# Add and GELU on one core: y's wide rest issued from ScalarE's queue, beside x's first half in SyncE's

## The chip, the cores and the metric

The kernel runs on one core of a Trainium2 chip. The metric is device time in microseconds (us). The kernel before takes 120.19 us (median of 3 runs, 120.18 to 120.26).

## The reference

```python
batch, dim = 1024, 4096          # x, y: float32
z = x + y
return 0.5 * z * (1 + np.tanh(np.sqrt(2 / np.pi) * (z + 0.044715 * z ** 3)))
```

Two arrays of 16.8 MB are read and one is written, 50.33 MB in all.

## The kernel before

**Layout.** Each array is spread over 128 partitions with 32,768 float32 columns each (`TOT`), in two halves of 16,384 columns (`HALF`). A half of an array is one contiguous 8.39 MB block of memory, in which each partition owns a row of 64 KB. In SBUF there is a tile `zt` for all of x, in which z and the result are made in place, and a tile `yt` that holds one half of y at a time. The second half of y goes into the same place as the first, so it can be loaded only when all adds of the first half are done.

**Transfers.** Seven DMAs move everything. x comes in two halves. y comes as a narrow first piece of 704 columns (352 KB), a wide rest of its first half (15,680 columns, 7840 KB), and the second half. The output goes out in two halves. All seven are issued by SyncE, in this order, which is the list `sp` (line 178):

```python
sp = [(load_y, 0), (load_y, 1), (load_x, 0), (load_x, 1), (load_y, 2)]
sp += [(store, i) for i in range(len(stores))]
```

The first four wait for nothing. `load_y(2)` waits for the adds of the first half, each store for the GELUs of its half. After the program is compiled, `begin_early(nc, 2)` moves SyncE's first two DMAs ahead of the barrier with which the body of the program begins.

**Compute.** The columns are cut into 20 chunks. For each, x and y are added (`add`, line 159) and GELU is applied (`gelu`, line 171). Chunks 0 to 8 are the first half. VectorE does most adds, and GpSimd chunks 7, 8 and 12. For eight chunks ScalarE first copies x into PSUM (`copy`, line 152), and VectorE's add reads it from there; PSUM has room for two chunks of 2048 columns, so a later copy waits until the add of an earlier chunk has read its place. The order on each engine is written out by hand: ScalarE's is `on_scalar` (line 107), five copies of the first half, two GELUs, three copies of the second half, and then the other GELUs. The loop at line 200 emits the instructions from these queues in turn; it doesn't reorder a queue.

Before the queues, a one-element activation on ScalarE (line 199) loads the GELU table.

Of the kernel before, what the change touches and what calls it, by code (L numbers as in the profile page):

```python
# [66 lines left out]
def kernel(  # L67
# [12 lines left out]
    nc = tc.nc  # L80
# [10 lines left out]
    def rows(array, lo, hi):  # L91
        flat, at = array.rearrange("n d -> (n d)"), 0
        for f, e in blocks:
            if f <= lo and hi <= e:
                own = flat[P * at : P * (at + e - f)].rearrange("(p c) -> p c", p=P)
                return own[:, lo - f : hi - f]
            at += e - f
        raise AssertionError((lo, hi))
# [8 lines left out]
    on_scalar = [("copy", c) for c in (2, 3, 4, 5, 6)] + [("gelu", 0), ("gelu", 1)] + [("copy", c) for c in (9, 10, 11)] + [("gelu", c) for c in range(2, 20)]  # L107
# [21 lines left out]
    yt = pool_y.tile([P, HALF], fp32, tag="y", name="y")  # L129
# [11 lines left out]
    def load_y(i):  # L141
        a, b = yr[i]
        o = a % HALF
        nc.sync.dma_start(out=yt[:, o : o + b - a], in_=rows(y, a, b))  # L144

    def store(i):
        a, b = sr[i]
# [25 lines left out]
    def earlier_user(c):  # L173
        lo, hi = copies[c], copies[c] + chunks[c]
        before = [k for k in copies if k < c and copies[k] < hi and copies[k] + chunks[k] > lo]
        return [(add, k) for k in before]

    sp = [(load_y, 0), (load_y, 1), (load_x, 0), (load_x, 1), (load_y, 2)]
    sp += [(store, i) for i in range(len(stores))]
    pool = [(add, c) for c in on_gpsimd]  # L180
    dve = [(add, c) for c in on_vector]
    acts = [(gelu if what == "gelu" else copy, c) for what, c in on_scalar]

    needs = {
        load_x: lambda i: [],
# [1 line left out]
        copy: lambda c: [(load_x, i) for i in over(xr, *cr[c])] + earlier_user(c),  # L187
        add: lambda c: [(load_x, i) for i in over(xr, *cr[c])]
        + [(load_y, i) for i in over(yr, *cr[c])]
        + [(copy, k) for k in copies if k == c]  # L190
        + [(add, k) for h, k in held.items() if h == c],
# [55 lines left out]
```

## Time and profile before

| | |
|---|---|
| median of 3 runs | 120.19 us |
| the profiled execution | 120.31 us |
| its span, first to last instruction | 118.8 us |
| DMA queues that carry data | 1, 98.5% of 16 engines' span |
| mean rate over the span | 424 GB/s |
| VectorE, ScalarE, GpSimd busy | 29.1, 44.1, 13.8 us |
| y's narrow piece, issue to landing | 3.0 us |
| y's wide rest, issue to landing | 21.7 us |
| x's first half landed | 41.47 us from the span's start |
| y's second half issued, landed | 55.02, 80.14 us |
| first store issued | 77.33 us |

The busy times of the compute engines are a third of the span or less; times in the table from the third block on are counted from the span's start or from the issue of the DMA, as said. A DMA's time from issue to landing includes the time in which it stands behind others in its queue.

### The profile page before, as it was taken

The page shows a single profiled execution, that of the slowest core. Times are in us where ns is not written, and L with a number is a line of the kernel's source. Part 1 is how long each engine was busy: PE and PEld are TensorE (multiplying, and loading weights), DVE is VectorE, ACT ScalarE, POOL GpSimd, SP SyncE. Part 2 cuts the span into 40 slices and gives each one's busy share as a digit, 9 for nine tenths or more (in the row PEclk, how much of TensorE's full clock was granted, in tenths as well). Part 3 has the DMA queues.
Part 4 walks back from the last instruction along what each step waited for, and adds up shares of the span by engine and source line. Part 5 has one row for each costly group of instructions (what it writes and reads, how often), then busy time and mean ns, then how long its engine had stood idle before and what let it go on. Part 6 is the DMA issues. An engine that isn't in the chain of part 4 may idle for free.

```text
span 118.8 us, 115 instructions
## 1 busy us (share of the span) xinstructions
DVE 29.1 (24%) x18; ACT 44.1 (37%) x30; POOL 13.8 (12%) x7
## 2 busy tenths in 40 slices
DVE  0000000000000099994000000009999930000000
ACT  4000000000000096893049999903799990000000
POOL 0000000000000019980000000009500000000000
DMA  9779977998889988998899888998899888988891
GB/s 459 338 338 422 591 338 338 507 552 353 353 353 662 397 353 353 574 485 353 353 441 618 353 353 353 640 419 353 353 552 507 353 353 353 706 353 353 353 640 66
DMA packets 1008, 50.33 MB, mean 424 GB/s; under 512 B 112, under 2 KB 112, under 8 KB 240
## 3 DMA queue, kind: packets, MB, share of 16 engines
q1 hardware_dynamic: 1008, 50.33, 98.5%
HBM read 33.55 MB, written 16.78 MB: 424 GB/s over the span
## 4 chain that ended last, share of the span: by engine, by line
DMA 55%; DVE 14%; ACT 10%; DVEq 1%; ACTq 0%; issue 0%; SPq 0%
DMA z<-in_x_dram 34%; DMA y<-in_y_dram 21%; DVE z L159 14%; ACT z L171 10%; DVEq L214 1%; ACTq L214 0%; DVEq L159 0%; SPq L144 0%
## 5 line engine op out<-in xcount | busy, mean ns | idle before, releaser
L171 ACT ACTIVATE z<-z 128x2048 f32<-128x2048 f32 (+3 forms) x20 | 29.7, 1555 | 5.4 <-DVE z L159 5.4
L152 ACT COPY ps<-z 128x2048 f32<-128x2048 f32 (+2 forms) x8 | 13.0, 1654 | 47.0 <-DMA z<-in_x_dram 45.3
L159 DVE TENSOR_TENSOR z<-z,y 128x2048 f32<-128x2048 f32 (+2 forms) x9 | 13.6, 1571 | 40.2 <-DMA z<-in_x_dram 40.2
L159 DVE TENSOR_TENSOR z<-ps,y 128x2048 f32<-128x2048 f32 (+2 forms) x8 | 15.6, 2014 | 25.3 <-DMA y<-in_y_dram 25.3
L159 POOL TENSOR_TENSOR z<-z,y 128x2048 f32<-128x2048 f32 x3 | 13.5, 4533 | 70.8 <-DVE z L159 43.6
L199 ACT ACT_TABLE_LOAD x1 | 1.3, 1283 | 1.3 <-PEq L231 1.3
L198 DVE MEMSET one<- 128x1 f32 x1 | 0.1, 59 | 1.3 <-PEq L231 1.3
L199 ACT ACTIVATE one<-one 128x1 f32<-128x1 f32 x1 | 0.2, 202 | 0.0
L231 POOL MEMSET const-float32-0.0<- 128x1 f32 x1 | 0.1, 99 | 0.2 <-issue 0.2
L231 POOL MEMSET const-bfloat16-1.0<- 128x1 bf16 x1 | 0.1, 102 | 0.0
L231 POOL MEMSET const-uint8-127<- 128x1 uint8 x1 | 0.1, 102 | 0.0
L231 POOL MEMSET const-float32-1.0<- 128x1 f32 x1 | 0.1, 99 | 0.0
## 6 DMA issues: line engine op xcount, KB each, us to landing
y<-in_y_dram SPq DMA_DIRECT2D x1, 7840.0 KB, 21.7
y<-in_y_dram SPq DMA_DIRECT2D x1, 352.0 KB, 3.0
z<-in_x_dram SPq DMA_DIRECT2D x2, 49.7
out_dram<-z SPq DMA_DIRECT2D x2, 21.6
y<-in_y_dram SPq DMA_DIRECT2D x1, 25.1
```

The source lines that it names most:

```text
L152: nc.scalar.copy(out=in_psum(c), in_=zt[:, a:b])
L159: ins = eng.tensor_add(out=zt[:, a:b], in0=first, in1=yt[:, o : o + b - a])
L171: nc.scalar.activation(out=zt[:, a:b], in_=zt[:, a:b], func=act.Gelu_apprx_tanh)
L198: nc.vector.memset(one[:, :1], 0.0)
L199: nc.scalar.activation(out=one[:, :1], in_=one[:, :1], func=act.Gelu_apprx_tanh)
L214: tc.compile()
L231: nc = _bacc.Bacc("TRN2", target_bir_lowering=False, num_devices=1)
```

## The change

`load_y(1)`, the wide rest of y's first half, is taken out of SyncE's list and put at the head of ScalarE's, and it is issued from ScalarE's DMA queue. There it follows the one-element activation of line 199 and precedes the first PSUM copy. SyncE's list now begins with y's narrow piece and x's first half, and these are the two that `begin_early` moves ahead of the barrier. All sizes, chunks, waits of the adds and the order of the compute stay as they are.

```diff
     def load_y(i):
         a, b = yr[i]
         o = a % HALF
-        nc.sync.dma_start(out=yt[:, o : o + b - a], in_=rows(y, a, b))
+        queue = nc.scalar if i == 1 else nc.sync
+        queue.dma_start(out=yt[:, o : o + b - a], in_=rows(y, a, b))
 
...
-    sp = [(load_y, 0), (load_y, 1), (load_x, 0), (load_x, 1), (load_y, 2)]
+    sp = [(load_y, 0), (load_x, 0), (load_x, 1), (load_y, 2)]
     sp += [(store, i) for i in range(len(stores))]
     pool = [(add, c) for c in on_gpsimd]
     dve = [(add, c) for c in on_vector]
-    acts = [(gelu if what == "gelu" else copy, c) for what, c in on_scalar]
+    acts = [(load_y, 1)] + [(gelu if what == "gelu" else copy, c) for what, c in on_scalar]
```

## The prediction

> **What bounds the kernel now.** I read the page from part 3 on, then the chain of waits, the timeline and a table of windows cut at the landings.
>
> ```profile
> DMA packets 1008, 50.33 MB, mean 424 GB/s; under 512 B 112, under 2 KB 112, under 8 KB 240
> q1 hardware_dynamic: 1008, 50.33, 98.5%
> ```
>
> One queue carries everything, and its packets fill 98.5% of 16 engines' span. The counts give the size of a piece. Seven DMAs on 16 engines have 112 small completion packets; 240 - 112 = 128 are the narrow first DMA of y; 1008 - 240 = 768 are left for six wide DMAs, 128 each, 8 for each engine.
>
> ```profile
> 41.50 0.05 DVEq L159
> 41.60 13.36 DVE z L159 x7
> 55.02 25.12 DMA y<-in_y_dram
> 84.85 11.86 ACT z L171 x7
> ```
>
> From the chain in order of time I take three landings and one issue. x's first half has landed at 41.47 (the wait before the adds ends there), the seven VectorE adds run to 54.96, y's second half is issued at 55.02 and lands at 80.14. The chain view calls these 13.36 us of DVE a part of the critical chain, but they lie beside x's second half, as the timeline of waits shows:
>
> ```profile
> 46.20 1.87 ACT L152 COPY ps<-z 128x2048 f32<-128x2048 f32 x1 [1.03 <-DVE z L159]
> 60.91 3.76 ACT L152 COPY ps<-z 128x512 f32<-128x512 f32 x3 [6.52 <-DMA z<-in_x_dram]
> 77.33 20.78 SPq L148 DMA_DIRECT2D out_dram<-z  x2
> ```
>
> ScalarE waits 6.52 us until x's second half has landed (about 60.83). So y's second half, issued at 55.02, stands in the queue for up to 5.8 us, and the first store, issued at 77.33, stands behind it for up to 2.8 us. The compute sets when y's second half can be issued, but not when it arrives. The windows say the same in bytes. I cut them at the landings: 3.0 and 0.42 + 21.7 from the DMA issue rows, 41.47 and 80.14 from the chain, 60.83 as ScalarE's wait ends at 60.91 less a hand-over of 0.08, and for the first store twice the issue row's median of 21.6 less the second store's 21.0, so 22.2 after 77.33.
>
> ```profile
> 3.00:22.14 19.14, 0.00 (x0) 0.00 (x0) 0.00 (x0) 1.00 0.99 422
> 22.14:41.47 19.33, 0.00 (x0) 0.00 (x0) 0.00 (x0) 1.00 1.00 434
> 41.47:60.83 19.36, 13.35 (x7) 11.21 (x7) 9.02 (x2) 1.00 1.00 433
> 60.83:80.14 19.31, 0.00 (x0) 16.39 (x10) 0.00 (x0) 1.00 1.00 434
> 80.14:99.48 19.34, 15.69 (x10) 15.01 (x11) 4.53 (x1) 1.00 1.00 434
> ```
>
> From one landing to the next it is 19.3 us per 8192 KB, whatever runs beside it, the last column in GB/s. Only the first window is off pace: its 7840 KB should take 7840/8192 x 19.33 = 18.50 us and take 19.14, an excess of **0.64 us**. That excess and the first microseconds are all the slack the transfers have. A piece is 19.33/8 = **2.42 us**.
>
> **The change, part by part.** SyncE loses one issue. Its rows are 0.33 to 0.42 us each. The first two DMAs of SyncE are hoisted ahead of the entry barrier; they were both of y's, and become y's narrow one and x's first half. So x's first half is issued at about 0.4 instead of 1.25, and x's second half at 1.25 instead of about 1.66. Neither is worth anything: the 16 engines have y's narrow DMA in hand until about 3.0 and 19 us of x behind it, so no engine is idle for want of an issue.
>
> ScalarE gains one issue, 0.33 to 0.42 us, behind the warm-up activation, whose row ends at 2.55 + 0.20 = 2.75. Queued behind it is the first PSUM copy, which waits for x's first half anyway: "ACT L152 COPY ... [38.75 <-DMA z<-in_x_dram]". Cost 0; uncovered it would be 0.4 us. The DMA waits for no semaphore.
>
> Next, when y's wide rest lands. From issue to landing y's narrow DMA took 3.0 us, of which its 352 KB are 0.83 us at pace, so the lag is at most 2.17. Issued by 3.2, the wide rest has its first piece ready between 3.2 and 5.3, while x's first half starts behind the narrow DMA at 2.2 to 3.0. x thus leads by one or two pieces of 2.42 us. If engines then take turns piece by piece, a lead of one means x's first half lands near 39 and y's rest near 41.5; a lead of two lets one piece of x's second half in ahead of y's last one: y lands at 41.47 + 2.42 = 43.9. If they share byte by byte, y's 0.34 MB fewer make up most of the lead and it lands between these. The adds need both, so they start 0 to 2.42 us later. ScalarE's first two copies are then done early, which saves nothing, since the VectorE row (13.36 us without a gap) is already limited by its own adds. GpSimd's two adds shift with them and end 1.9 us before VectorE (53.06 against 54.96).
>
> The delay ends at y's second half: issued at 55.0 to 57.4, with at most 2.17 lag it is ready by 59.6, and x's second half still lands at 60.83 because the same bytes have gone before it. Slack left: at least 60.83 - 59.6 = 1.2 us. ScalarE's slack falls from 6.52 to at least 4.1. Everything after 60.83 is unchanged.
>
> A rule of the Trainium skill bears on the taking of turns. "DMA: Bandwidth & Descriptors", section "Queues, rings and completion order", says that each DMA engine goes round-robin between queues and switches only at packet boundaries. Nothing in this trace shows it, as it has one data queue; by it, with a piece as a packet, the sum is the one above.
>
> What the sharing does to the pace is the one price that no row shows. The nearest rows bound it: 434 GB/s in the windows of x, 422 in the window of y. Bounded below: the excess of 0.64 goes away, -0.64. Bounded above: both streams run as y's did, x's 19.33 us gain 0.67 more; or twice that for two switches per pair, 1.3. I take 0, by the five windows that hold pace whichever tensor and direction they carry.
>
> Sum: 0 (SyncE) + 0 (ScalarE) + 0 (delay inside the slack) + 0 (pace) on the profiled execution: 120.31, of which 118.8 is the span and 1.5 lies around it. The median of the runs is 0.12 below that execution, so the forecast is 120.2. A second queue could also need setting up outside the span; no row shows that, and I put it at 0 as well.
>
> **The rivals.** *The excess goes (faster).* x's pieces now begin the stream and y's come between them. If the excess belongs to y's wide rest being read alone, up to 0.64 goes: 119.55; half of it gives 119.9. For it: only that DMA is off pace, and x's, y's second half and both stores are not. Against it: it is also the first wide DMA of the run, and whatever starts the stream may pay the same.
>
> *The sharing costs pace (slower).* Every engine alternates between two tensors for 38 us. At y's excess for both streams: +0.67, 120.9; at double that 121.5. It decides from 0.24 us on, that is 0.24/16 = 15 ns per piece over 16 pieces, little beside 2420 ns. For it: the transfers bound the kernel everywhere, so each lost nanosecond is seen at the end. Against it: 434 GB/s held while engines passed from one DMA to the next. The Trainium skill has a rule in this direction: the same page, section "Latency and other measured facts", reports that DMA rows at a pitch of a large power of two can run at half rate. No run here shows that for two tensors; the 64 KB pitch inside one tensor runs at 434.
>
> *y's rest lands too late (slower).* If x's queue has three or more pieces committed when y's arrive, y's rest is 4.84 us late or more, and y's second half misses its place: ready at 55.02 + 4.84 + up to 2.17 = 62.0, so up to 1.2 us of idle engines; with four pieces up to 3.6. That gives 121.4 to 123.8. It decides when the adds start over 3.6 to 5.8 us late. For: nothing in the trace says how deep an engine commits. Against: the lead is a matter of 1 to 3 us by the issue rows.
>
> *One queue is emptied before the other (slower, and the change then doesn't run the two side by side).* x's second half stands behind the first in SyncE's queue from 2 us on. If the engines stay with that queue, y's rest comes after both and lands at 60.83; adds to 74.3; y's second half issued at 74.4 with nothing else to move, landing at 74.4 + 19.33 + 2.1 = 95.8 instead of 80.14: about 15.7 more, 135.9. By the Trainium skill's account on the same page a packet may hold up to 64 descriptors; x's two halves are 18 pieces with their completions, so it does not exclude this. If turns are taken whole DMA by whole DMA instead, y merely trades places with x's first half, lands at 41.5, and nothing changes; that belongs to the forecast.
>
> **How the numbers follow.** No change 0.40; excess goes 0.20; pace lost 0.26; late rest 0.09; one queue first 0.05. A difference under 0.2% (0.24 us) is about what a measurement of this kernel cannot tell from no change. The first case is within it, the second faster, the other three slower: 0.20, 0.40, 0.40. The likeliest single case gives 120.2, its own range 119.95 to 120.45. Eight in ten need the second and third cases with their bounds: 119.6 to 121.6, which leaves out the late and the one-queue case and a little of the third.
>
> **What would show it.** Right: two data queues in part 3; ScalarE's first copy waits for x near 39, the first VectorE add for y's rest between 41.4 and 44; y's second half issued by 57.5; landings near 60.8 and 80.1; all windows after that at 434 GB/s. The excess going shows as x's second half landing near 60.2. Lost pace shows as its landing after 61.1 with no idle DMA slice. A late rest shows as a DMA slice well under 9 tenths near 61 us. One queue first shows as adds that begin after 60. Wrong would be a difference that arises after 61 us or outside the span.

## The result and the profile after

The changed kernel takes 120.97 us (median of 5 runs, 120.91 to 121.42) against 120.25 for the kernel before beside it: a ratio of 1.0069, 95% interval 1.0057 to 1.0080, so **0.7 us slower**. The time lies in the forecast's range, and it went the way of the slower cases; the likeliest single case, no change, did not happen. The profiled execution is the slowest of the five, 121.42 with a span of 119.9, so its rows overstate the typical loss by about 0.4 us.

Part 3 of the page shows the second queue, with y's wide rest in it:

```profile
DMA packets 1008, 50.33 MB, mean 420 GB/s; under 512 B 112, under 2 KB 112, under 8 KB 240
q1 hardware_dynamic: 864, 42.30, 82.1%
q10 hardware_dynamic: 144, 8.03, 15.5%
```

The timeline of the changed kernel, the rows at which something is issued or a transfer awaited (start, duration, instruction, idle time before it and what ended that):

```profile
1.43 0.37 ACTq L145 DMA_DIRECT2D y<-in_y_dram  x1
39.21 3.67 ACT L153 COPY ps<-z 128x2048 f32<-128x2048 f32 x2 [36.46 <-DMA z<-in_x_dram]
44.05 2.36 DVE L160 TENSOR_TENSOR z<-z,y 128x1024 f32<-128x1024 f32 x2 [42.67 <-DMA y<-in_y_dram]
57.48 0.33 SPq L145 DMA_DIRECT2D y<-in_y_dram  x1
60.92 3.76 ACT L153 COPY ps<-z 128x512 f32<-128x512 f32 x3 [4.07 <-DMA z<-in_x_dram]
77.34 21.87 SPq L149 DMA_DIRECT2D out_dram<-z  x2
```

x's first half is there at 39.2 and y's wide rest at 43.9. The adds begin 2.45 us later than before, y's second half is issued at 57.48 instead of 55.02, and ScalarE's slack before x's second half falls from 6.52 to 4.07. So far it is what a lead of two pieces was to give. x's second half also lands where it did (60.84; 60.83 before). The windows, cut at the landings of this kernel, show where the time went:

```profile
2.89:39.19 36.30, 0.00 (x0) 0.00 (x0) 0.00 (x0) 1.00 0.99 423
39.19:43.93 4.74, 0.00 (x0) 3.67 (x2) 0.00 (x0) 1.00 1.02 442
43.93:60.84 16.91, 13.35 (x7) 7.54 (x5) 9.02 (x2) 1.00 0.99 430
60.84:81.24 20.40, 0.00 (x0) 16.39 (x10) 0.00 (x0) 1.00 0.96 414
81.24:100.59 19.35, 15.70 (x10) 15.01 (x11) 4.53 (x1) 1.00 1.00 434
100.59:119.90 19.31, 0.00 (x0) 0.00 (x0) 0.00 (x0) 1.00 0.88 380
```

Only the window of y's second half is long: 20.40 against 19.31, at 414 GB/s against 434. The excess of 1.09 us is the whole difference of the two spans (119.9 - 118.8). While the two queues take turns, up to 43.9, nothing is lost.

The trace's packet records show this window engine by engine. (They carry no engine's number; I put each piece behind the one that ends where it begins.) Fifteen engines pass from x's last piece to y's first without a gap, and their y lands between 79.59 and 80.14, just as before. One engine is free at 60.28 and begins y's second half only at 61.15, 0.87 us idle; its first piece takes 0.07 longer than 2.42, its last one 0.37. It lands at 81.24. All engines have the same bytes to move, so it never catches up, and the others don't gain either. The chain shows what the others wait for:

```profile
57.48 23.76 DMA y<-in_y_dram
85.95 11.86 ACT z L172 x7
97.81 0.52 ACTq L215
98.33 0.52 ACT z L172
```

From y's landing to the end of the last GELU it is 17.6 us, in both kernels. The second store can be issued at 98.85 (98.33 + 0.52) instead of 97.74, and the first pieces of it begin at 99.72 instead of 98.63. In the kernel before the first engine was free at 98.52 and waited 0.12 us, so this step had no reserve, and the other 15 engines now wait 0.6 to 1.3 us. The time doesn't hang on that wait, however: the late engine goes from its first store piece to its last without a gap and ends alone at 119.56, when the others have ended by 119.22. In the kernel before the last engine ended at 118.44, 1.12 earlier.

### The profile page after: what moved, and what is told of

It is laid out like the page before. It is cut to its first block, busy times and chain, and to the rows that moved or that the text cites. A ratio compares the mean times of both kernels' runs of the same rounds, so it can differ in the third digit from the quotient of the medians.

```text
span 119.9 us, 115 instructions
## 1 busy us (share of the span) xinstructions
DVE 29.1 (24%) x18; ACT 44.1 (37%) x30; POOL 13.8 (11%) x7
## 4 chain that ended last, share of the span: by engine, by line
DMA 55%; DVE 14%; ACT 10%; DVEq 1%; ACTq 0%; issue 0%; SPq 0%
DMA y<-in_y_dram 55%; DVE z L160 14%; ACT z L172 10%; DVEq L215 1%; ACTq L215 0%; ACT L200 0%; DVEq L160 0%; SPq L145 0%
```

## The experiments

Theory A: y's second half is issued too close to its turn because y's wide rest lands late. Theory B: it is the two queues themselves that cost the time. Each kernel ran 4 to 11 times beside the kernel before (median 120.19 to 120.22 there); ratios are to it, with 95% intervals.

**The change once more.** No edit.

> The changed kernel once more, to see whether its loss has one place. Theory A (late order): y's wide rest lands 2.4 us late, the adds end late, y's second half is issued at 57.5 instead of 55.0, and on one of the 16 engines its pieces arrive too late; that engine stands idle and nothing later gives the time back. Theory B (two queues): taking turns between two queues, or having a second one, costs the time, wherever y's second half is issued. Both expect 120.9 to 121.1. A expects again x's second half landing at 60.8 as in the kernel before and y's second half landing 0.5 to 1.2 us late.

120.81 us, ratio 1.0046 (1.0033 to 1.0059).

```profile
60.76:80.76 20.00, 0.00 (x0) 16.39 (x10) 0.00 (x0) 1.00 0.97 419
```

Again it is this window that is long, by 0.69 against 19.31. This time no engine idles by more than 0.13 us at its start; instead the first pieces of y's second half, begun at 59.8 to 60.4, take 0.1 to 0.7 us more than 2.42 on 14 of the 16 engines. The place is the same, the form differs. One thing upstream differs too: one engine gave x a lead of one piece instead of two, so that ScalarE's first copy began only at 41.39; y's wide rest still landed at 43.75 and y's second half was issued at 57.30.

**One queue, y's second half held back by 2.5 us.** In the kernel before, VectorE first does three adds into a scratch tile, as soon as x's first half is there (the edit in part):

```diff
+    def idle(n):
+        w = n[1]
+        nc.vector.tensor_add(out=one[:, :w], in0=zt[:, HALF - w : HALF], in1=zt[:, HALF - w : HALF])
...
-    dve = [(add, c) for c in on_vector]
+    dve = [(idle, n) for n in [(0, 694), (1, 694), (2, 694)]] + [(add, c) for c in on_vector]
```

> One queue, as before the change, but VectorE does three extra adds of 694 columns (2.45 us in all, into a scratch tile) before its first add, so that the first half's adds end and y's second half is issued 2.45 us later, near 57.5. A: slower by the same 0.7 us as the change, 120.9 to 121.1, with x's second half landing at 60.8 and y's second half 0.5 to 1.1 us late. B: no change, 120.2, as there is only one queue.

121.01 us, ratio 1.0074 (1.0054 to 1.0094): the change's whole loss, without the change. y's second half is issued at 57.52. Windows:

```profile
41.37:60.69 19.32, 15.90 (x10) 11.21 (x7) 9.02 (x2) 1.00 1.01 434
60.69:81.42 20.73, 0.00 (x0) 16.39 (x10) 0.00 (x0) 1.00 0.94 405
```

x's second half is at pace, y's second half loses 1.4 us in the profiled execution (121.6, the slowest of its runs). Its records have three first pieces longer by 0.5 us, two of them after 0.2 us of idle time, and three last ones longer by 0.3 to 0.65. This is A's outcome: the loss needs no second queue.

**Held back by less and by more.** The same edit with `[(0, 495), (1, 495)]` and with four adds of 771 columns.

> One queue; two extra adds of 495 columns hold the first half's adds back by about 1.2 to 1.4 us, so y's second half is issued near 56.4, some 3.5 us before the first engine is done with x's second half. Theory A (late order) with a price of about 0.7 us at 2.5 us of lead and none at 4.9: between, 0 to 0.4 us slower, 120.2 to 120.6. Theory B (two queues): 120.2.

> The same with four adds of 771 columns, about 3.6 to 4 us: y's second half is issued near 58.9, 1.0 us before the first engine is done. A: the loss grows with each microsecond, 1.5 to 2.3 us slower, 121.7 to 122.5, and all 16 engines stand idle near 60. B: 120.2. The bound of the prediction (2.17 us from issue to first piece) would give 1.1 us at most, 121.3.

The short hold issues y's second half at 56.16 and costs nothing: 120.22, ratio 1.0002 (0.9994 to 1.0011). The long one issues it at 58.75 and costs 3.5 us: 123.68, ratio 1.0295 (1.0273 to 1.0317), more than A had expected. The window of y's second half in each:

```profile
60.72:80.06 19.34, 0.00 (x0) 16.39 (x10) 0.00 (x0) 1.00 1.00 434
```

```profile
60.67:83.27 22.60, 0.00 (x0) 16.39 (x10) 0.00 (x0) 1.00 0.99 418
```

The first engine is free near 59.8 to 59.9 in all of these. So a lead of 4.9 us (before) or 3.7 us costs nothing, 2.3 to 2.5 us (the middle hold, the change in both its runs) costs 0.6 to 0.8, and 1.1 us costs 3.5. The loss doesn't stop at the idle time of the start: in the long hold the last pieces too run 0.07 to 1.5 us over on 15 of the 16 engines.

**x's second half behind y's rest.** In the changed kernel (written short; `acts` on the right is ScalarE's list of the kernel before, and `load_x` picks its queue as `load_y` does):

```diff
-    sp = [(load_y, 0), (load_x, 0), (load_x, 1), (load_y, 2)]
+    sp = [(load_y, 0), (load_x, 0)]
+    acts = [(load_y, 1), (load_x, 1)] + acts[:7] + [(load_y, 2)] + acts[7:]   # all three on nc.scalar
```

> The change, and x's second half and y's second half are issued from ScalarE's queue as well, so that no piece of x's second half can go ahead of the last pieces of y's wide rest. The two queues still take turns over x's first half and y's wide rest. A: y's rest lands near 41.5, y's second half is issued near 55.0, and the time is that of the kernel before, 120.1 to 120.4. B: 120.9 or more, as 14 turns are taken as in the change.

121.03 us, ratio 1.0074 (1.0062 to 1.0086). The time is B's, but the windows are A's up to 80 us:

```profile
60.66:79.96 19.30, 0.00 (x0) 16.39 (x10) 0.00 (x0) 1.00 1.04 435
79.96:100.17 20.21, 15.69 (x10) 15.01 (x11) 4.53 (x1) 1.00 0.96 415
```

y's rest lands at 41.27, y's second half is issued at 54.82 and loses nothing. A new loss of 0.9 us appears behind it: the first pieces of the first store, alone in SyncE's queue since 39, take 0.6 to 1.0 us over. To tell whether the turns had a hand in that, the stores were moved to ScalarE's queue too (in part):

```diff
-    sp += [(store, i) for i in range(len(stores))]
+    acts = [(load_y, 1), (load_x, 1)] + acts[:7] + [(load_y, 2)] + acts[7:17] + [(store, 0)] + acts[17:] + [(store, 1)]
```

> The run with x's second half behind y's wide rest in ScalarE's queue, with the two stores moved to that queue as well, so that nothing follows in another queue. There y's second half had landed on time and the first store's first pieces took 0.7 to 1.0 us longer than 2.42. If that came from the store standing alone in a queue that had run empty: 120.1 to 120.4, first store landing 19.3 us behind y's second half. If taking turns costs time (theory B), or the loss lies in the store itself: 120.9 to 121.1 again. Theory A says only that y's second half lands on time.

120.24 us, ratio 1.0005 (0.9996 to 1.0014). The two queues take the same turns over the first 40 us as in the change, and the time is that of the kernel before.

```profile
60.93:80.33 19.40, 0.00 (x0) 16.39 (x10) 0.00 (x0) 1.00 1.00 432
80.33:99.65 19.32, 15.70 (x10) 15.01 (x11) 4.53 (x1) 1.00 1.00 434
```

**y's second half in two DMAs.** In the changed kernel, so that turns and the landing at 43.8 stay as they are and the lead grows (in part; SyncE's list gets the fourth load of y):

```diff
-    yloads = [704, 15680, HALF]
+    yloads = [704, 15680, 2048, HALF - 2048]
```

> The change, with y's second half in two DMAs: 2048 columns, which need only the first two chunks' adds and can be issued near 46.5, and the rest, issued near 57.5 as now, with 2.4 us more work ahead of it. The two queues take turns as in the change and y's wide rest lands at 43.9 as there. A: the loss goes, 120.1 to 120.4. B: 120.9 as in the change.

120.28 us, ratio 1.0005 (0.9996 to 1.0013).

```profile
43.96 2.36 DVE L160 TENSOR_TENSOR z<-z,y 128x1024 f32<-128x1024 f32 x2 [42.58 <-DMA y<-in_y_dram]
46.35 11.37 SPq L145 DMA_DIRECT2D y<-in_y_dram  x2
80.17 2.29 DVE L160 TENSOR_TENSOR z<-ps,y 128x2048 f32<-128x2048 f32 x1 [14.53 <-DMA y<-in_y_dram]
```

y's wide rest still lands at 43.83. The wide part of y's second half is issued at 57.38, as late as in the change, but its first piece has its turn only at 62.28, behind the 2048 columns: a lead of 4.9 us. It lands at 80.08 (80.14 in the kernel before), and the loss is gone.

**A wider first piece of y**, with two queues and with one:

```diff
-    yloads = [704, 15680, HALF]
+    yloads = [2048, 14336, HALF]
```

> The change, with y's first piece 2048 columns wide and its rest 14336. The first piece keeps the engines busy until about 4.5 us, so that the rest and x's first half begin together and the rest, which is an eighth smaller, is done first. A: the adds start when x's first half has landed, 41.5 to 42, y's second half is issued at 55.0 to 55.6, and the time is 120.1 to 120.4. B: 120.9 as in the change.

> The kernel before with one queue and y's first piece 2048 columns wide, to see whether the small gain of the run with the wide first piece and two queues comes from the piece or from the queues. If from the piece: 119.9 to 120.1; if from the queues: 120.2.

Two queues: 120.08, ratio 0.9989 (0.9981 to 0.9998), where B expected 120.9. One queue: 119.94, ratio 0.9983 (0.9974 to 0.9991), the fastest kernel here. The gain comes from the piece, not from the queues. In the records the wide pieces begun before 20 us are over their time by 0.46 us per engine in the kernel before (0.25 to 0.33 in the three holds) and by 0.02 and 0.01 in these two; x's second half lands at 60.28 and 60.31 instead of 60.83. Most of it is lost again in y's second half (windows of the run with two queues):

```profile
41.11:60.28 19.17, 13.24 (x7) 11.03 (x7) 9.03 (x2) 1.00 1.01 438
60.28:80.08 19.80, 0.00 (x0) 16.40 (x10) 0.00 (x0) 1.00 0.98 424
```

One of its last pieces, begun at 76.82, is 0.49 us over, near the issue of the first store at 76.78. I took this for a store issued too late for its turn, and issued it earlier.

**The first store early.** One queue, wide first piece, and

```diff
-    on_scalar = [copies 2-6] + [("gelu", 0), ("gelu", 1)] + [copies 9-11] + [("gelu", c) for c in range(2, 20)]
+    on_scalar = [copies 2-6] + [("gelu", c) for c in range(9)] + [copies 9-11] + [("gelu", c) for c in range(9, 20)]
```

(written short). The second kernel also has `stores = [HALF, HALF - 4096, 4096]`, the third that and the change's two queues.

> One queue, y's first piece 2048 wide, and ScalarE does the GELUs of the first half ahead of the three copies of the second half, so that the first store is issued near 67 instead of 76.8. In the wide run x's second half landed 0.5 us early and y's second half lost it again in a last piece begun at 76.9, right after the first store was issued. Theory A carried over (a DMA issued less than about 2.5 us ahead of its turn costs time, whichever it is): y's second half lands near 79.6, 119.4 to 119.8. If the stretched piece has another cause: 119.9 to 120.1 as in the wide run.

> The same, and the second store is cut into 12288 and 4096 columns, of which the first can be issued 4 us earlier, ahead of the engines' end of the first store. A carried over: no idle time near 98 us, 119.2 to 119.7. Without it: as the run without the cut.

> The same with the change: y's rest (14336 columns) is issued from ScalarE's queue. A: two queues cost nothing where every DMA is issued in time, so within 0.2 us of the run with one queue. B: 0.7 us above it.

All three are slower than the kernel before, which no time expected of the first one allowed for: 121.29 (1.0086, 1.0072 to 1.0099), 121.31 (1.0092, 1.0076 to 1.0107) and 121.27 (1.0085, 1.0071 to 1.0099). The chain and the window of the first:

```profile
54.45 26.72 DMA y<-in_y_dram
```

```profile
60.36:81.17 20.81, 0.00 (x0) 9.70 (x7) 0.00 (x0) 1.00 1.00 403
```

The store is issued at 66.4, ten microseconds ahead, and now the last piece of y's second half is over by 1.3 to 1.6 us on every engine. In the two kernels with the cut store it is over by 0.5 to 0.95, with smaller excesses ahead of it, and y lands as late (81.13 with one queue). No engine computes between 70.1 and 81.2 us in the first run, so the new order on ScalarE doesn't stretch these pieces while they run. So theory A does not carry over to a store that follows a load. The kernel before agrees: its first store was issued at 77.33, 1.9 us before the first engine was free, and nothing was lost. That the early issue is what costs is the likely reading, but it is not shown: the edit moved the GELUs as well, and no run issued the store early by itself. That the first two and the third agree within their intervals says once more that two queues cost no pace.

## Why the prediction was right in its range and wrong in its likeliest case

**The order of turns** was right, one detail excepted. The queues alternate piece by piece with a lead of two for x: the records run x, x, y, x, y and so on, each piece at 2.42 or 2.31 us. This agrees with the round-robin of the Trainium skill, "DMA: Bandwidth & Descriptors", section "Queues, rings and completion order". The page calls 9 to 17 descriptors typical for the packet that an engine finishes before it switches; here the records change queue after every single piece. The detail: y's last piece does not come behind a piece of x's second half, as the prediction had it. All pieces of y's rest are done by 40.6 to 41.2. What comes late is the small completion packet behind them, at 43.0 to 43.6: it has a turn of its own, and a piece of x's second half goes ahead of it. x's first half shows the same, done by 36.5 and announced at 38.3 to 38.8. Where x's second half is in y's own queue, y's completions follow the last piece at once (on the first engine of that run the piece ends and the completion begins at 40.53).

**The price of the delay** is the step that failed. "With at most 2.17 lag it is ready by 59.6" set a slack of at least 1.2 us and a price of 0. Two sizes in it were off. The slack was counted to 60.83, the landing on the last engine; by the records the engines were free from 59.9 to 60.5. And the lag was taken from y's narrow DMA, which meets idle engines: in the profiled execution of the change one engine's first piece began 3.67 us after the issue (61.15 - 57.48). On busy engines a lead of 2.3 to 2.5 us already costs 0.6 to 0.8 us, and the holds put the safe lead between that and 3.7. So the rival "y's rest lands too late" had the right mechanism with the wrong threshold (adds over 3.6 us late; 2.45 was enough) and too high a price (1.2 us and more). That the measured time lies in the range is luck as far as the mechanism goes: the range reached up to 121.6 for the sake of lost pace, which the runs exclude, and was drawn to leave the late rest out.

**The step from y's landing to the last store** was left out. "Everything after 60.83 is unchanged" holds only while all 16 engines deliver y's second half on time. The latest engine sets the end by its own delay, and the 17.6 us from y's landing to the last GELU's end, with no reserve before the last store, make the other 15 nearly as late.

**The other rivals.** *The sharing costs pace* came nearest in time, 120.9, by a mechanism that isn't there: where only the lead differs, the loss goes (120.28) and comes without a second queue (121.01). *The excess goes* did not happen in the change, since x's second half lands at 60.84; it does happen with the wider first piece, and there it is not due to the queues. *One queue is emptied first* is excluded by the records. SyncE's and ScalarE's issues cost nothing, as forecast, but ScalarE's is issued at 1.43, not at 2.75: it does not wait for the warm-up activation queued ahead of it.

Not settled: why the loss at a short lead takes the form of an idle engine in one execution and of longer pieces in the next, and what lengthens the last load pieces when the store is issued early. A wide first piece with the first store issued at the old 77.3 was not tried; it would be the next step from 119.94.

## What to carry to other kernels

When transfers set the time, ask of each DMA with how much lead it is issued before its turn, not only whether it is issued before the queue runs dry: here 3.7 us was enough and 2.5 was not. The second queue cost no pace here, but it moved landings: a DMA counts as landed only when its completion has had its turn, up to one piece of the other queue later, and what waits for it is issued later by as much. A test that holds one issue back in the unchanged kernel separates such a cause from the change itself.

## What the runs showed of the hardware that was not expected

- Completion packets take turns between queues like pieces of data: 2.4 us behind the last byte here, one 64 KB piece.
- A load that follows a load in a busy queue needs a lead: none lost at 3.7 us, 0.6 to 0.8 us lost at 2.3 to 2.5, 3.5 at 1.1.
- With a store queued 10 us ahead behind a load, the load's last piece was longer on all 16 engines, by 1.3 to 1.6 us in one run and by 0.5 to 0.95 in two. With the store issued at about the time when that piece began, nothing was lost in the kernel before (77.3), and the last piece was up to 0.45 and 0.49 us longer on an engine in the two runs with the wide first piece (76.8). In a queue that had stood empty, beside loads in the other one, the store's own first pieces were 0.6 to 1.0 us longer.
- The Trainium skill, "DMA: Bandwidth & Descriptors", section "Issuing engines are not separate DMA queues", says that issuing from several engines saves only issue time. The pace agrees (120.24 with turns over 40 us, 120.22 without). The landings moved all the same: the later of the two that the adds wait for came at 43.93 instead of 41.47.
